# Three issuers changed in one trunk layer: pins out of the DeltaNet heads, x1 stores and operand-set loads on GpSimd

## The chip, the cores and the metric

The kernel runs on one core of a Trainium2 chip. The metric is device time of one launch in microseconds. Three runs of the kernel before gave 1958.57, 1965.72 and 1967.81 us (median 1965.72). One more execution was recorded by the hardware profiler; every row below is from it.

## The reference

One decoder layer on x of 1024 positions by 1024 channels, all in float32:

```
h = rmsnorm(x, norm1_g) * (1 + scale1(c)) + shift1(c)
x = x + gate1(c) * hybrid_mixer(h)          # DeltaNet, pooling, spatial gating, retention, gates, w_out
h = rmsnorm(x, norm2_g) * (1 + scale2(c)) + shift2(c)
x = x + gate2(c) * (square(relu(h @ mlp_w1)) @ mlp_w2)
out = rmsnorm(x, final_g)
```

The mixer's DeltaNet has 4 heads of 128 channels; for each, q, k and v pass a causal convolution, then a chunked gated delta rule with a triangular solve per chunk of 64. The MLP widens 1024 channels to 4096 and back.

## The kernel before, in words

The work runs in stages on one core: modulation and the pooling and spatial branches (to about 200 us), the four DeltaNet heads (to about 545), retention (710), the sigmoid gates (1020), the branch products (1205), the output projection (to 1297), and the MLP (to the end). Channels lie on partitions and positions along the free axis, in two halves of 512.

A float32 product is made as three fp32r matmuls: each operand is cast to a high part by ScalarE and the rest subtracted by VectorE (`split` and `put`, lines L112 and L113, and L967 and L968). In the MLP one level of Strassen is used on top: 7 products of 12 matmuls each take the place of 8. Its operands, sums and differences of the four quarters, are "operand sets": b11, b21, n2, t3, n1, t4, b22.

**The order of the work.** Program order on each engine is set by a scheduler that knows data, slots and costs. `keep_in_program_order` holds an instruction where the source writes it (a "pin"). `fill(n)` takes n matmuls (L424) from a projection that has nothing to do with this head, and writes them there, so that TensorE has work while the head's chain on VectorE and ScalarE goes on. In `dn_mix` 10 fillers stand ahead of the pinned key transposes (L575), and in head 0 another 28 ahead of the pinned key-query products (L615). L601 are the key-key products, L608 the value transposes, L591 the VectorE step that scales the transposed keys `kt` and frees their bank. `dn_inverse` is the triangular solve, a row of 31 pairs of small VectorE instructions (L652 and L656); for the next head its first pair is made before the scan of the head at hand (`next(nxt)`), and pinned.

**The output projection** (`outproj`) makes for each half eight blocks of x1: load the residual `xr` (L1200), multiply, add on VectorE (L1204), store x1 to DRAM for later (L1206). All DMAs there are issued by SyncE in one queue, which goes on to the loads of the MLP's first weights, `raw<-in_w` (L1250). `xr` and the squares of the norm share a ring of slots named "st", six or seven tiles of 128x512.

**The MLP** makes 16 panels of the hidden activation (`up`), and stores the seven operand sets of each panel to DRAM (`ad_b`, `ad_n`, `ad_t`, L1285; their names in the trace merge b11, b21 and b22, n1 and n2, t3 and t4). Its second product (`down`) runs over four chunks c of four panels, and within a chunk over four output blocks m; the seven sets of a chunk stay in SBUF for its four blocks. While the last block of a chunk is multiplied, each set that has been used up is replaced by that of the next chunk: 4 loads of 256 KB (L1414, tile `ar`, in the six slots of "st"), each cast on ScalarE (L967) and subtracted on VectorE (L968). Such a "turn" has 28 loads; there are four, in panel 15 for chunk 0 and in the last blocks of chunks 0, 1 and 2, and 112 loads in all. SyncE issues them in one queue with the stores of the sets (L1285), the weight loads (L1250) and, in chunk 1, the reloads of x1 (L1536).

Of the kernel before, what the change touches and what calls it, by code (L numbers as in the profile page):

```python
# [13 lines left out]
ALU = mybir.AluOpType  # L14

P = 128
# [84 lines left out]
class Trunk:  # L101
# [460 lines left out]
    def dn_mix(self, h, q, kT, vT, Es):  # L562
        nc, mp = self.nc, self.mp
        sm = lambda n: mp.tile([P, 8], FP32, tag=n, name=n, bufs=2)
        kk, qq, bb, bk, nn, tmp = sm("kk"), sm("qq"), sm("bb"), sm("bk"), sm("nn"), sm("nt")
        kt = mp.tile([P, NB, P], FP32, tag="kt", name="kt", bufs=2)
        nv = mp.tile([P, NB, P], FP32, tag="vt", name="nv", bufs=2)
        N3 = mp.tile([P, NB, P], FP32, tag="N3", name="N3", bufs=2)
        Ab = mp.tile([P, NB, P], FP32, tag="Ab", name="Ab", bufs=2)
        cb = lambda t, c: t[:, c * P:(c + 1) * P]  # L570
        qT = q[3][1]
        pks = [self.pss() for _ in range(2)]
        self.fill(10)
        for c in range(NB):
            i = nc.tensor.transpose(out=pks[c // 4][:, c % 4 * P:(c % 4 + 1) * P], in_=cb(kT, c), identity=self.ident)  # L575
            if c == 0:
                self.tc.keep_in_program_order(i)
        for c in range(NB):
            junk = mp.tile([P, P], FP32, tag="junk", name="junk", bufs=1)
            nc.scalar.activation(out=junk, in_=pks[c // 4][:, c % 4 * P:(c % 4 + 1) * P], func=AF.Square,  # L580
                                 accum_out=kk[:, c:c + 1])
        q[2]()
        q2 = mp.tile([P, T], FP32, tag="r4", name="q2", bufs=3)
        nc.scalar.activation(out=q2, in_=qT, func=AF.Square)
        nc.vector.tensor_scalar_add(out=kk, in0=kk, scalar1=EPS)
        nc.vector.reciprocal(out=bb, in_=kk)
        nc.vector.tensor_tensor(out=bb, in0=bb, in1=self.beta[:, h], op=ALU.mult)
        nc.vector.tensor_tensor(out=bk, in0=bb, in1=self.ekl[:, h], op=ALU.mult)
        for hf in range(2):
            c4 = slice(4 * hf, 4 * hf + 4)  # L590
            nc.vector.tensor_tensor(out=kt[:, c4], in0=pks[hf].rearrange("p (c d) -> p c d", c=4),  # L591
                                    in1=self.b4(bk[:, c4]), op=ALU.mult)
            nc.gpsimd.tensor_tensor(out=Es[hf], in0=Es[hf], in1=self.b4(bb[:, c4]), op=ALU.mult)
        self.rsqrt(kk, nn, tmp)
        nc.vector.tensor_tensor(out=nn, in0=nn, in1=kk, op=ALU.mult)
        for hf in range(2):
            c4 = slice(4 * hf, 4 * hf + 4)
            ch = range(4 * hf, 4 * hf + 4)
            p1 = self.pss()
            for j in range(4):  # L600
                nc.tensor.matmul(out=p1[:, j * P:(j + 1) * P], lhsT=cb(kT, ch[j]), rhs=cb(kT, ch[j]), start=True, stop=True)  # L601
            nc.vector.tensor_tensor(out=N3[:, c4], in0=p1.rearrange("p (c i) -> p c i", c=4), in1=Es[hf], op=ALU.mult)
        for hf in range(2):
            c4 = slice(4 * hf, 4 * hf + 4)
            ch = range(4 * hf, 4 * hf + 4)
            pv = self.psm()
            for j in range(4):
                nc.tensor.transpose(out=pv[:, j * P:(j + 1) * P], in_=cb(vT, ch[j]), identity=self.ident)  # L608
            nc.vector.tensor_tensor(out=nv[:, c4], in0=pv.rearrange("p (c d) -> p c d", c=4), in1=self.b4(nn[:, c4]),
                                    op=ALU.mult)  # L610
            p2 = self.pss()
            if h == 0 and hf == 0:
                self.fill(28)
            for j in range(4):
                i = nc.tensor.matmul(out=p2[:, j * P:(j + 1) * P], lhsT=cb(kT, ch[j]), rhs=cb(qT, ch[j]), start=True,  # L615
                                     stop=True)
                if h == 0 and hf == 0 and j == 0:
                    self.tc.keep_in_program_order(i)
            nc.vector.tensor_tensor(out=Ab[:, c4], in0=p2.rearrange("p (c i) -> p c i", c=4), in1=Es[hf], op=ALU.mult)
        self.drain()  # L620
        for hf in range(2):
            sl = slice(hf * 512, (hf + 1) * 512)
            qs = [mp.tile([P, 512], FR, tag="w5", name=n, bufs=4) for n in ("qh", "ql")]
            self.split(q2[:, sl], *qs)
            pq = self.pss()
            for i, r in enumerate(qs):
                nc.tensor.matmul(out=pq[0:1], lhsT=self.oner, rhs=r, start=(i == 0), stop=(i == 1))
            nc.scalar.copy(out=q2[0:1, sl], in_=pq[0:1])
        qd = self.dp.tile([1, T], FP32, tag="qd", name="qd", bufs=2)
        nc.sync.dma_start(out=qd, in_=q2[0:1])  # L630
        nc.sync.dma_start(out=qq, in_=qd.rearrange("o (c p) -> (o p) c", p=P))

        nr = mp.tile([P, 32, 32], FP32, tag="nr", name="nr")
        nd = self.dp.tile([4, 8, 32, 32], FP32, tag="nd", name="nd", bufs=2)
        for b in range(4):
            nc.sync.dma_start(out=nd[b].rearrange("c j i -> j c i"), in_=N3[b * 32:b * 32 + 32, :, b * 32:b * 32 + 32])
        nc.sync.dma_start(out=nr.rearrange("p j i -> p (j i)"),
                          in_=nd.rearrange("b c j i -> (b c) (j i)").unsqueeze(0).broadcast_to([4, 32, 1024]))
        return dict(h=h, q=qT, k=kT, kt=kt, nv=nv, N3=N3, Ab=Ab, qq=qq, nr=nr)

    def dn_inverse(self, s):

        nc, mp = self.nc, self.mp
# [5 lines left out]
        for j in range(31):  # L649
            m = 31 - j  # L650
            tmp = mp.tile([P, 31, 8], FP32, tag="ttm", name="ttm", bufs=1)
            i = nc.vector.tensor_tensor(out=tmp[:, :m], in0=nr[:, j, j + 1:].unsqueeze(2).broadcast_to([P, m, 8]),  # L652
                                        in1=tt[:, j:j + 1].broadcast_to([P, m, 8]), op=ALU.mult)
            if j == 0 and s["h"]:
                self.tc.keep_in_program_order(i)
            nc.vector.tensor_tensor(out=tt[:, j + 1:], in0=tt[:, j + 1:], in1=tmp[:, :m], op=ALU.subtract)  # L656
            yield
        t2 = mp.tile([P, 8, 32], FP32, tag="t2", name="t2")
# [213 lines left out]
    def mixers(self):  # L872
# [22 lines left out]
        self.fillers = [vn[0]]  # L895
        st = self.dn_mix(0, q, k[3][1], v[3][1], E)
        prev = None
        nxt = self.dn_inverse(st)
        for h in range(4):
            inv = nxt  # L900
            hooks = {}
            if prev:
                hooks[12] = lambda: self.mix_out(0, h - 1, *prev)
            if h < 3:
                k, q = self.dn_proj(1, h + 1), self.dn_proj(0, h + 1)
                v = vn
                v[1]()
                hooks[30] = v[2]
                self.run(k[0], hooks, inv, 2)
                k[1]()  # L910
                self.run(q[0], {12: k[2]}, inv, 2)
                for _ in inv:
                    pass
                q[1]()
                E = self.dn_decay(h + 1)
                z, zg = self.gate_in(DZ + h)
                self.fillers = [zg]
                sn = self.dn_mix(h + 1, q, k[3][1], v[3][1], E)
                vn = self.dn_proj(2, h + 2) if h < 2 else self.ret_proj(2, 0)
                self.fillers = [vn[0]]  # L920
            else:
                rk, rq = self.ret_proj(1, 0), self.ret_proj(0, 0)
                self.run(rk[0], hooks, inv, 2)
                self.run(rq[0], {}, inv, 2)
                for _ in inv:
                    pass
                z, zg = self.gate_in(DZ + h)
                self.fillers = [zg]
            self.dn_levels(st)
            if h < 3:  # L930
                nxt = self.dn_inverse(sn)
                next(nxt)
            prev = self.dn_scan(h, st), self.prm[:, R_DNG:R_DNG + 1], z
            if h < 3:
                st = sn
# [250 lines left out]
    def outproj(self):  # L1186
# [7 lines left out]
        for hf in range(2):  # L1194
            x1 = self.x1[hf] = self.xb.tile([P, NB, 512], FP32, tag="b16", name="x1", bufs=4)
            ssq = self.st("ssq")
            for db in range(NB):
# [5 lines left out]
                         [self.ml[hf][:, k] for k in range(NB)])  # L1203
                nc.vector.scalar_tensor_tensor(out=x1[:, db], in0=ps, scalar=self.modc[:, 16 + db:17 + db], in1=xr,  # L1204
                                               op0=ALU.mult, op1=ALU.add)
                nc.sync.dma_start(out=self.x1d[hf][db], in_=x1[:, db])  # L1206
                self.sumsq(x1[:, db], ssq, db, nc.vector if db == NB - 1 else nc.gpsimd)
                if hf == 1:
                    self.h2_first(db, rs)
# [63 lines left out]
    def mlp(self):  # L1273
# [134 lines left out]
        def load(c, o):  # L1408
# [2 lines left out]
                self.S2[o] = self.opset(pool, tag, 1 if tag == "ex" else 4)  # L1411
            for j in range(4):
                r = self.st("ar")
                nc.sync.dma_start(out=r, in_=ad[o, 4 * c + j])  # L1414
                self.put(self.S2[o], j, r)

        for p in range(NP):
# [232 lines left out]
```

## Time and profile before

| | before |
|---|---|
| runs, us | 1958.57, 1965.72, 1967.81 |
| profiled execution, us | 1969.17 |
| its span, us | 1967.3 |
| mean granted TensorE clock | 0.980 |
| TensorE matmul busy | 1878.3 us, 95% |
| VectorE busy | 1343.7 us, 68% |
| ScalarE busy | 762.5 us, 39% |
| GpSimd busy | 116.5 us, 6% |

Busy time is the time in which an engine had an instruction under way. "PE" is TensorE's matmuls, "DVE" VectorE, "ACT" ScalarE, "POOL" GpSimd, "SP" SyncE, and "SPq" its queue of DMA issues. PEclk is the granted share of TensorE's full clock; at half of it a busy engine does half of the work. A row "A <- B" says that A's idle time ended with B.

### The profile page before, as it was taken

The page shows a single profiled execution, that of the slowest core. Times are in us where ns is not written, and L with a number is a line of the kernel's source. Part 1 is how long each engine was busy: PE and PEld are TensorE (multiplying, and loading weights), DVE is VectorE, ACT ScalarE, POOL GpSimd, SP SyncE. Part 2 cuts the span into 40 slices and gives each one's busy share as a digit, 9 for nine tenths or more (in the row PEclk, how much of TensorE's full clock was granted, in tenths as well). Part 3 has the DMA queues.
Part 4 walks back from the last instruction along what each step waited for, and adds up shares of the span by engine and source line. Part 5 has one row for each costly group of instructions (what it writes and reads, how often), then busy time and mean ns, then how long its engine had stood idle before and what let it go on. Part 6 is the DMA issues. An engine that isn't in the chain of part 4 may idle for free.

```text
span 1967.3 us, 24099 instructions
## 1 busy us (share of the span) xinstructions
PE 1878.3 (95%) x8888; PEld 1537.7 (78%) x8888; DVE 1343.7 (68%) x2337; ACT 762.5 (39%) x1214; POOL 116.5 (6%) x105
## 2 busy tenths in 40 slices
PE   5999989999999998999999999989999999999997
PEld 2788867777788887888878888878778877787875
DVE  7844687787454468566655776558886666788785
ACT  4523543442312134434442123545234444635542
POOL 4100300210000000000000000200000000000000
PEclk9999999998899999999999999999999999999998
DMA  7522111231122224454448653535664564535422
GB/s 267 185 98 86 53 37 45 60 84 48 49 75 61 68 102 160 150 182 166 166 157 267 197 191 130 182 134 177 200 203 133 185 199 155 204 131 190 151 85 86
DMA packets 142225, 270.67 MB, mean 138 GB/s; under 512 B 45078, under 2 KB 45718, under 8 KB 138012
## 3 DMA queue, kind: packets, MB, share of 16 engines
q1 hardware_dynamic: 140188, 262.85, 40.1%
q0 software_dynamic: 1920, 6.29, 1.3%
q8 instruction: 69, 1.13, 0.2%
q14 instruction: 48, 0.39, 0.1%
HBM read 198.30 MB, written 66.60 MB: 135 GB/s over the span
## 4 chain that ended last, share of the span: by engine, by line
PE 42%; DMA 5%; DVE 4%; issue 2%; ACT 2%; SPq 0%; DVEq 0%; ACTq 0%
PE sm L985 14%; PE mm L985 14%; PE mm L128 9%; PE sm L128 4%; DMA ar<-ad_b 2%; DVE op L968 1%; DVE x L1277 1%; DMA ar<-ad_t 1%; DVE x L1276 1%; ACT op L967 1%; DMA ar<-ad_n 1%; DVE raw L1256 1%; DMA raw<-in_w 1%; DVE dl L113 0%; DMA adaw<-in_ada 0%
## 5 line engine op out<-in xcount | busy, mean ns | idle before, releaser
L424 PE MATMUL mm<-hh,wlo 128*128 128x512 f32 x512 | 207.4, 405 | 0.0
L424 PE MATMUL mm<-hl,whi 128*128 128x512 f32 x512 | 206.9, 404 | 0.0
L424 PE MATMUL mm<-hh,whi 128*128 128x512 f32 x512 | 206.8, 404 | 0.0
L113 DVE TENSOR_TENSOR wlo<-raw,whi 128x1024 fp32r<-128x1024 f32 x71 | 87.6, 1236 | 96.4 <-ACT whi L112 95.6
L112 ACT CAST whi<-raw 128x1024 fp32r<-128x1024 f32 x73 | 76.5, 1050 | 178.5 <-PE mm L424 109.8
L985 PE MATMUL sm<-op,ch 128*128 128x512 f32 x392 | 123.1, 395 | 1.7 <-ACT v L1487 1.7
L985 PE MATMUL mm<-op,gh 128*128 128x512 f32 x352 | 112.8, 400 | 9.2 <-ACT x L1368 4.9
L424 PEld LDWEIGHTS mm<-hh,whi 128*128 128x128 f32 x512 | 98.4, 192 | 18.1 <-issue 0.3
L424 PEld LDWEIGHTS mm<-hh,wlo 128*128 128x128 f32 x512 | 98.4, 192 | 17.6
L424 PEld LDWEIGHTS mm<-hl,whi 128*128 128x128 f32 x512 | 98.1, 192 | 17.8
L112 ACT CAST gh<-raw 128x1024 fp32r<-128x1024 f32 x58 | 61.1, 1053 | 113.3 <-PE sm L985 72.9
L985 PE MATMUL sm<-op,gh 128*128 128x512 f32 x328 | 102.3, 393 | 2.6 <-DVE x L1276 1.5
L112 ACT CAST ch<-raw 128x1024 fp32r<-128x1024 f32 x57 | 60.0, 1053 | 85.7 <-PE sm L985 48.9
L985 PEld LDWEIGHTS sm<-op,ch 128*128 128x128 f32 x392 | 73.7, 190 | 19.8 <-ACT v L1487 2.6
L985 PEld LDWEIGHTS mm<-op,gh 128*128 128x128 f32 x352 | 67.0, 192 | 26.1 <-ACT x L1368 5.8
L985 PE MATMUL mm<-op,ch 128*128 128x512 f32 x272 | 84.9, 394 | 0.0
L1256 DVE TENSOR_TENSOR raw<-raw 128x512 f32<-128x512 f32 (+1 forms) x96 | 83.2, 866 | 1.6
L968 DVE TENSOR_TENSOR op<-ar,op 128x512 fp32r<-128x512 f32 x112 | 72.1, 687 | 16.6 <-ACT op L967 16.3
L113 DVE TENSOR_TENSOR cl<-raw,ch 128x1024 fp32r<-128x1024 f32 x57 | 69.6, 1222 | 18.2 <-ACT ch L112 17.8
L985 PE MATMUL sm<-op,cl 128*128 128x512 f32 x196 | 77.2, 394 | 0.6 <-DVE cl L113 0.6
L967 ACT CAST op<-ar 128x512 fp32r<-128x512 f32 x112 | 66.2, 618 | 29.2 <-DMA ar<-ad_b 16.3
L985 PEld LDWEIGHTS sm<-op,gh 128*128 128x128 f32 x328 | 60.8, 188 | 18.6 <-DVE x L1276 4.0
(463 smaller groups left out, 4671.9 us busy)
## 6 DMA issues: line engine op xcount, KB each, us to landing
raw<-in_wt SPq DMA_DIRECT2D x80, 512.0 KB, 5.3
raw<-in_w SPq DMA_DIRECT2D x32, 1024.0 KB, 4.8
adaw<-in_ada SPq DMA_DIRECT2D x64, 256.0 KB, 5.6
sig<-sg SPq DMA_DIRECT2D x64, 256.0 KB, 2.7
sg<-x SPq DMA_DIRECT2D x60, 256.0 KB, 2.2
ad_b<-x SPq DMA_DIRECT2D x48, 256.0 KB, 2.3
ar<-ad_b SPq DMA_DIRECT2D x48, 256.0 KB, 5.4
adaw<-in_ada SPq DMA_DIRECT2D x16, 512.0 KB, 7.1
```

The source lines that it names most:

```text
L112: nc.scalar.copy(out=hi, in_=raw)
L113: (eng or nc.vector).tensor_tensor(out=lo, in0=raw, in1=hi.bitcast(FP32), op=ALU.subtract)
L128: self.nc.tensor.matmul(out=ps, lhsT=a, rhs=b, start=(i == 0), stop=(i == 3 * n - 1))
L424: self.nc.tensor.matmul(out=ps, lhsT=blk(a, k), rhs=r[hf][:, k], start=(k == 0 and i == 0), stop=(k == NB - 1 and i == 2))
L967: self.nc.scalar.copy(out=hi, in_=x)
L968: self.nc.vector.tensor_tensor(out=lo, in0=x, in1=hi.bitcast(FP32), op=ALU.subtract)
L985: self.nc.tensor.matmul(out=ps, lhsT=a, rhs=b, start=start and n == 0, stop=(n == 11), skip_group_check=True)
L1256: add = lambda o, a, b: nc.vector.tensor_tensor(out=o, in0=a, in1=b, op=ALU.add)
L1276: tt = lambda eng, o, a, b, op: eng.tensor_tensor(out=o, in0=a, in1=b, op=op)
L1277: stt = lambda o, a, s, b, op0, op1: nc.vector.scalar_tensor_tensor(out=o, in0=a, scalar=s, in1=b, op0=op0, op1=op1)
```

## The change

(A) `fill(10)` and `fill(28)` go, with the pins on L575, L615 and the first solve pair; the next head's solve is no longer started ahead of the scan. (B) The 16 stores of x1 are issued by GpSimd. (C) So are the 112 loads of operand sets.

```
@@ dn_mix
-        self.fill(10)
         for c in range(NB):
-            i = nc.tensor.transpose(out=pks[c // 4][:, c % 4 * P:(c % 4 + 1) * P], in_=cb(kT, c), identity=self.ident)
-            if c == 0:
-                self.tc.keep_in_program_order(i)
+            nc.tensor.transpose(out=pks[c // 4][:, c % 4 * P:(c % 4 + 1) * P], in_=cb(kT, c), identity=self.ident)
...
-            if h == 0 and hf == 0:
-                self.fill(28)
             for j in range(4):
-                i = nc.tensor.matmul(out=p2[:, j * P:(j + 1) * P], lhsT=cb(kT, ch[j]), rhs=cb(qT, ch[j]), start=True,
-                                     stop=True)
-                if h == 0 and hf == 0 and j == 0:
-                    self.tc.keep_in_program_order(i)
+                nc.tensor.matmul(out=p2[:, j * P:(j + 1) * P], lhsT=cb(kT, ch[j]), rhs=cb(qT, ch[j]), start=True, stop=True)
@@ dn_inverse
-            if j == 0 and s["h"]:
-                self.tc.keep_in_program_order(i)
@@ heads
-        nxt = self.dn_inverse(st)
         for h in range(4):
-            inv = nxt
+            inv = self.dn_inverse(st)
...
-            if h < 3:
-                nxt = self.dn_inverse(sn)
-                next(nxt)
@@ outproj
-                nc.sync.dma_start(out=self.x1d[hf][db], in_=x1[:, db])
+                nc.gpsimd.dma_start(out=self.x1d[hf][db], in_=x1[:, db])
@@ mlp, load
-                nc.sync.dma_start(out=r, in_=ad[o, 4 * c + j])
+                nc.gpsimd.dma_start(out=r, in_=ad[o, 4 * c + j])
```

Line numbers after the change are lower: L575, L601, L608 and L615 become L574, L598, L605 and L610; L1200, L1206 and L1250 become L1186, L1192 and L1236; L1285 and L1414 become L1271 and L1400.

In the heads, TensorE's order in head 0 before; the names `hh`, `hl`, `whi` and `wlo` are those of the fillers, and L627 is the next step of the head:

```order
L424 MATMUL mm<-hh,whi 128x512
L575 MATMUL sm<-cst,cv 128x128 x8
L601 MATMUL sm<-cv 128x128 x8
L608 MATMUL mm<-cst,cv 128x128 x4
L424 MATMUL mm<-hl,whi 128x512
...
L615 MATMUL sm<-cv 128x128 x4
L608 MATMUL mm<-cst,cv 128x128 x4
L615 MATMUL sm<-cv 128x128 x4
```

and the same place after:

```order
L574 MATMUL sm<-cst,cv 128x128 x8
L605 MATMUL mm<-cst,cv 128x128 x8
L424 MATMUL mm<-hh,whi 128x512
...
L598 MATMUL sm<-cv 128x128 x8
L424 MATMUL mm<-hh,wlo 128x512
...
L610 MATMUL sm<-cv 128x128 x8
```

Before, 10 fillers stand ahead of the transposes and 28 between L608 and L615 (12 there in head 1). After, none stands ahead, 5 stand ahead of the key-key products and 17 between these and L610, in heads 0, 1 and 3 alike. The count of matmuls is the same.

At the end of the output projection, SyncE's queue before:

```order
L1206 DMA x1d_4_9913<-x_10241 128x512
L1200 DMA xr<-in_xT 128x512
L1206 DMA x1d_5_9914<-x_10241 128x512
L1200 DMA xr<-in_xT 128x512
L1206 DMA x1d_6_9915<-x_10241 128x512
L1200 DMA xr<-in_xT 128x512
L1206 DMA x1d_7_9916<-x_10241 128x512
L1250 DMA raw<-in_w 128x1024 x5
```

and after:

```order
L1186 DMA xr<-in_xT 128x512
L117 DMA raw<-in_wo 128x1024
L1186 DMA xr<-in_xT 128x512 x3
L1236 DMA raw<-in_w 128x1024 x5
L1271 DMA ad_b_0_10582<-x_10781 128x512
```

The stores x1d have left the queue, so that the last three residual loads stand together and the first MLP weights right behind them.

In panel 15, where the sets of chunk 0 are loaded, SyncE's queue before (`ad_b_15`, `ad_n_15` and `ad_t_15` are the stores of that panel, `sums` and `x` their sources):

```order
L1414 DMA ar<-ad_t_2_10664 128x512
L1285 DMA ad_b_15_10693<-x_13027 128x512
L1414 DMA ar<-ad_t_3_10665 128x512
L1414 DMA ar<-ad_b_0_10678 128x512
L1414 DMA ar<-ad_b_1_10679 128x512
L1285 DMA ad_b_15_10613<-x_12996 128x512
L1250 DMA raw<-in_w 128x2048
L1414 DMA ar<-ad_b_2_10680 128x512
L1414 DMA ar<-ad_b_3_10681 128x512
L1285 DMA ad_n_15_10661<-sums 128x512
```

and after:

```order
L1271 DMA ad_b_15_10597<-x_12923 128x512
L1271 DMA ad_b_15_10693<-x_13027 128x512
L1271 DMA ad_b_15_10613<-x_12996 128x512
L1236 DMA raw<-in_w 128x2048
L1271 DMA ad_n_15_10661<-sums 128x512
```

The loads stand in GpSimd's queue after, in the same order among themselves, with nothing between them up to the end of the MLP. The chunk in each number is the first figure behind the name: `ad_t_2` is panel 2.

## Rows read from the trace of the kernel before

**Rows 1.** The page: busy time by engine, and the software DMA queue.
```profile
PE 1878.3 (95%) x8888; PEld 1537.7 (78%) x8888; DVE 1343.7 (68%) x2337; ACT 762.5 (39%) x1214; POOL 116.5 (6%) x105
...
q0 software_dynamic: 1920, 6.29, 1.3%
```
**Rows 2.** Waits of TensorE, 1440 to 1900 us: total, times, longest.
```profile
PE mm L985 <- ACT x L1368: 4.9, 1, 4.9
PE mm L985 <- DVE al L113: 3.9, 1, 3.9
PE sm L985 <- ACT v L1487: 2.8, 3, 1.1
PE mm L985 <- ACT v L1487: 0.9, 1, 0.9
PE mm L985 <- ACT x L1484: 0.9, 1, 0.9
```
**Rows 3.** Windows: length, busy time and count by engine, PEclk, DMA share, GB/s.
```profile
1608.00:1618.00 10.00, 6.32 (x28) 4.88 (x26) 4.74 (x7) 6.00 (x11) 0.00 (x0) 1.00 0.85 296
1618.00:1626.00 8.00, 6.09 (x15) 4.31 (x16) 4.09 (x7) 3.99 (x8) 0.00 (x0) 0.57 0.41 131
1626.00:1636.00 10.00, 10.00 (x45) 7.98 (x44) 9.08 (x14) 6.23 (x11) 0.00 (x0) 1.00 0.59 203
1790.00:1796.00 6.00, 3.20 (x15) 2.31 (x13) 5.92 (x10) 4.28 (x7) 0.00 (x0) 0.98 0.91 324
1796.00:1803.00 7.00, 5.87 (x15) 4.67 (x16) 6.58 (x9) 0.00 (x0) 0.00 (x0) 0.53 0.35 135
```
**Rows 4.** The chain of waits up to the first turn's stall: start, length, what.
```profile
1602.14 0.45 issue
1602.59 0.70 DVE sums L1277
...
1603.31 0.32 SPq L1285
...
1603.68 6.15 DMA ar<-ad_b
...
1610.47 0.54 ACT x L1282
...
1611.03 0.32 SPq L1285
...
1611.45 4.07 DMA ar<-ad_n
```
**Rows 5.** The chain of waits, 1772 to 1802 us, by line.
```profile
by line: DMA ar<-ad_b 36.5%; DVE op L968 18.6%; DMA ar<-ad_t 11.5%; DMA ar<-ad_n 10.9%; PE sm L985 10.0%; PE mm L985 6.9%; ACT op L967 6.3%; issue 5.4%; DVE al L113 3.8%; ACT v L1487 2.3%; DVE x L1276 2.2%; DVEq L968 0.2%; ACTq L1487 0.1%
```
**Rows 6.** Tile ar: its casts, and microseconds from issue to landing of its loads.
```profile
L967 ACT CAST op<-ar x112: 604/621/627, 1562.0 to 1877.1; 128x512 fp32r<-128x512 f32 x112
L968 DVE TENSOR_TENSOR op<-ar,op x112: 681/685/694, 1563.5 to 1878.1; 128x512 fp32r<-128x512 f32 x112
...
DMA to landing us min/median/max: 2.7/4.0/6.1
```
**Rows 7.** Tiles hr, then sw, which GpSimd loads: issue, VectorE beside it, landing.
```profile
L1024 DVE TENSOR_TENSOR hr<-hr x8: 684/685/692, 714.5 to 742.8; 128x512 f32<-128x512 f32 x8
...
L1048 POOL DMA_DIRECT2D hr<-hd x4: 548/548/577, 660.4 to 734.7; - x4
...
DMA to landing us min/median/max: 2.9/3.0/4.2
...
DMA to landing us min/median/max: 3.0/3.6/6.6
```
**Rows 8.** Timeline of the output projection's end: start, length, engine, line.
```profile
1281.07 0.33 SPq L1206 DMA_DIRECT2D x1d<-x  x1
...
1297.76 8.35 SPq L1250 DMA_DIRECT2D raw<-in_w  x4
...
1300.02 0.26 ACT L1580 ACTIVATE rt<-mm,eps 128x4 f32<-128x4 f32 x1 [1.94 <-PE mm L1571]
...
1302.01 1.04 ACT L112 CAST ah<-raw 128x1024 fp32r<-128x1024 f32 x1 [1.73 <-DMA raw<-in_w]
...
1303.11 1.22 PE L985 MATMUL sm<-op,ah 128*128 128x512 f32 x2 [3.13 <-ACT ah L112]
```
**Rows 9.** Waits of TensorE in the heads, 200 to 545 us, and a window.
```profile
PE sm L615 <- DVE kt L591: 8.4, 2, 6.2
PE sm L681 <- DVE XX L687: 3.5, 1, 3.5
PE sm L601 <- ACT E L557: 2.1, 1, 2.1
...
276.00:284.00 8.00, 3.52 (x17) 3.55 (x18) 7.69 (x30) 2.73 (x3) 2.11 (x2) 0.57 0.02 4
```

More of the change, by code (lines that the diff above doesn't have):

```diff
@@ L638, in dn_mix @@
                           in_=nd.rearrange("b c j i -> (b c) (j i)").unsqueeze(0).broadcast_to([4, 32, 1024]))
-        return dict(h=h, q=qT, k=kT, kt=kt, nv=nv, N3=N3, Ab=Ab, qq=qq, nr=nr)
+        return dict(q=qT, k=kT, kt=kt, nv=nv, N3=N3, Ab=Ab, qq=qq, nr=nr)
     def dn_inverse(self, s):
@@ L651, in dn_inverse @@
             tmp = mp.tile([P, 31, 8], FP32, tag="ttm", name="ttm", bufs=1)
-            i = nc.vector.tensor_tensor(out=tmp[:, :m], in0=nr[:, j, j + 1:].unsqueeze(2).broadcast_to([P, m, 8]),
-                                        in1=tt[:, j:j + 1].broadcast_to([P, m, 8]), op=ALU.mult)
-            if j == 0 and s["h"]:
-                self.tc.keep_in_program_order(i)
+            nc.vector.tensor_tensor(out=tmp[:, :m], in0=nr[:, j, j + 1:].unsqueeze(2).broadcast_to([P, m, 8]),
+                                    in1=tt[:, j:j + 1].broadcast_to([P, m, 8]), op=ALU.mult)
             nc.vector.tensor_tensor(out=tt[:, j + 1:], in0=tt[:, j + 1:], in1=tmp[:, :m], op=ALU.subtract)
```

## The prediction

> **What bounds the kernel now.** I read the page first: TensorE is busy 1878.3 of 1967.3 us [rows 1]. So nothing that stays beside its matmuls can be worth much, and a gain has to come out of the 89 us in which it is idle or out of stretches at a low clock. Then TensorE's waits for the stages that the change touches, then windows around the longest ones, and last the chain of waits that leads up to them.
>
> In the MLP's second product the waits are few: 4.9, 3.9, 2.8, 0.9 and 0.9 us, 13.4 together [rows 2]. The two long ones cost more than they last. A full window of 10 us holds 45 matmuls, 0.222 us each. The 18 us from 1608 to 1626 hold 28 + 15 = 43 where 81 would fit, and the second of these windows was granted a clock of 0.57, the 1.2 GHz level for most of it, after the engine had stood still for 4.9 us. So this stall costs 38 x 0.222 = 8.4 us. The same for 1790 to 1803: 30 of 58, at 0.53 in its second part, 28 x 0.222 = 6.2 us [rows 3]. With the three short groups (2.8 + 0.9 + 0.9 = 4.6 us) the four turns cost 8.4 + 6.2 + 4.6 = 19.2 us. That is the ceiling for (C).
>
> **(C), the 112 loads.** What makes the first stall is the chain before it [rows 4]: a load of `ar` waits to be issued behind a store of panel 15 in SyncE's queue, and that store waits for VectorE or ScalarE, which is itself behind the cast of an earlier `ar`. The queue so turns a wait for a store into a wait for a load. From 1602.14 to 1603.68 (1.54 us) and from 1610.47 to 1611.45 (0.98 us) the chain goes through a store and not through a load, a cast or a slot: 2.5 us that GpSimd's queue, which has no store in it, doesn't have to wait. The load that lands late under this is one of six slots, and the later ones start from it, so 2.5 us is the least that comes off if landing times stay. With the stall cut from 4.9 to 2.4 us or less part of the slow clock goes too (8.4 - 4.9 = 3.5 us of the cost lie there). I take 2.5 + 3.5 = 6 us; bounds 2.5 and 8.4.
>
> At the second stall the chain is another one: 36.5 + 11.5 + 10.9 = 59% of it is landings of `ar`, and VectorE's `op` L968 another 19%; no store and no SyncE step appears in it [rows 5]. It is bound by six slots: a slot is taken for 4.0 us of landing, 0.62 of cast and 0.69 of subtraction, 5.3 us [rows 6], so 28 loads take at least 28 x 5.3 / 6 = 24.7 us, where seven products want 84 x 0.222 = 18.6. A new issuer adds no slot. It changes the landing alone: loads that GpSimd issues took 3.0 (hr) and 3.6 us (sw) as a median [rows 7] against 4.0. At 3.6 a turn takes 28 x 4.9 / 6 = 22.9 us, 1.8 less, at 3.0 it takes 20.1, 4.6 less; but hr and sw flew in stages with less other traffic, so I take a little under the smaller: 1.5 us for the second stall and 1 us for the short ones together. Bounds: the whole 10.8 us that they cost, and for the other side the worst landing of sw, 6.6 us, 28 x 2.6 / 6 = 12 us more in each of the three turns of `down`, 36 us in all.
>
> The issue itself costs GpSimd 548 ns a load [rows 7], 28 x 0.55 = 15.3 us in a turn, under the 18.6 us of its products, and GpSimd has nothing else to do there (0.00 busy [rows 3]). SyncE loses 28 issues a turn; its stores and weight loads go earlier, and may crowd the DMA engines (0.85 and 0.91 busy in the two bad windows [rows 3]); that is in the bound above. Sum for (C): -6 - 1.5 - 1 = -8.5 us.
>
> VectorE ran beside GpSimd's loads without stretching: its hr instructions took 684 to 692 ns there [rows 7], the same as L968's 681 to 694 without GpSimd [rows 6]. The Trainium skill (SBUF — State Buffer, the box "The DVE blocks DMA trap" in the section "SBUF: two separate sides") holds the opposite danger: GpSimd writes its DMAs' descriptors itself, and can't while VectorE runs an instruction in a two-port mode. By that rule loads would land late in the turns, and (C) would turn into a loss. The 3.0 and 3.6 us speak against it, though the 6.6 us at worst leaves it open; it is the first rival below. The skill also says (DMA: Bandwidth & Descriptors, "Issuing engines are not separate DMA queues") that a second issuer saves only sequencer time, small beside the transfer. By that rule (C) would be worth about nothing; here the sequencer's time is that of waits in order, and the 2.5 us of the first chain are of this kind.
>
> **(B), the 16 stores.** Before, SyncE's last store of x1 waits for the last block, and so the first MLP weights are issued at 1297.76 and used at 1302.01, 4.25 us later. After, the queue holds before them only three residual loads, the last of which takes the slot of the block whose store went at 1281.07. So the weights are issued some 15 us earlier and lie there. What ends last is then ScalarE's root at 1300.02, done at 1300.28; the cast starts there instead of at 1302.01, and TensorE's first product, which waits for that cast, 1.7 us before 1303.11 [rows 8]. The stores cost GpSimd 16 x 0.55 = 9 us beside its sums of squares, which have some 5.6 us from one block to the next (from the fifth store at 1281.07 to the queue's step past the eighth at 1297.76 [rows 8]). Gain 1.7 us; bounds 0 and 3.1 (the whole wait).
>
> **(A), the heads.** The matmuls stay; what matters is how many of them cover the chain up to `kt`. TensorE waited for it twice, 8.4 us, and the longest, 6.2 us, left a window at a clock of 0.57 [rows 9]. In head 1 10 + 12 = 22 fillers stood ahead of L615 before, and 5 + 17 = 22 stand there after. TensorE gets there at the same time, and VectorE, busy 7.69 of 8 us in that window, sets when `kt` is ready: no change. The 2.1 us wait of L601 gets 5 fillers, 1.1 us, ahead of it, but they are taken from what covers L615. In head 0 38 become 22, 16 x 0.222 = 3.6 us less cover, while the transposes start 10 x 0.222 = 2.2 us earlier; at most 1.4 us is short there. The early solve pair is one instruction of 62. I take 0; bounds: a gain of the two waits and the slow clock behind the longer (8.4 + 0.43 x 8 = 11.8 us), or a loss of one more such stall, 6.2 + 3.4 = 9.6 us.
>
> **The sum.** -8.5 - 1.7 + 0 = -10.2 us against the profiled execution's 1969.17, 1959.0 us. That execution lies 3.45 us above the median of the runs, and above the highest of them; the change is the same step from either, so I forecast from the median: 1965.7 - 10.2 = 1955.5 us.
>
> **Rivals.**
> 1. GpSimd's loads land later (slower). From 4.0 us each further microsecond costs a turn 28 / 6 = 4.7 us, the three turns of `down` 14 us. It decides from a landing of 4.0 + 10.2 / 14 = 4.7 us: above that the gain of all parts is gone. At 6 us, 28 - 10.2 = 18 us slower, 1983. For it: sw's worst of 6.6, DMA engines 0.85 to 0.91 busy there. Against: the medians 3.0 and 3.6. Chance 0.14.
> 2. The heads get longer (slower). One more stall such as that of head 1, 9.6 us, in two heads, 19 - 10 = 9 us slower, 1975. For it: in head 0 the cover shrinks. Against: the count of 22 in head 1 and a chain on VectorE that no filler moves. Chance 0.08.
> 3. No change: slots bound every turn, and the head of the queue was not what held the loads. Only (B) is left, 1964. For it: 59% landings in the second chain [rows 5]. Against: the two stores in the first [rows 4]. Chance 0.23.
> 4. The loads run so far ahead that every turn is covered: 19.2 + 1.7 = 21 us, 1945. For it: two of the four turns share less than the 4.6 us of short waits already [rows 2]. Against: 24.7 us of slots for 18.6 us of products. Chance 0.15.
>
> **How the numbers follow.** The forecast has 0.40: a gain of 5 to 15 us, 1951 to 1961. About 0.5%, 9.8 us, is what a measurement of this kernel can tell from no change; it cuts the forecast's case through the middle. Faster by more: 0.23 of the forecast, 0.15 of rival 4, and 0.05 of rival 3 where (A) gains; 0.43. Within: 0.17 of the forecast, 0.18 of rival 3, 0.04 of rivals 1 and 2; 0.39. Slower: the rest, 0.18. The range takes in rivals 3 and 4 and a part of 1 and 2: 1942 to 1976. The forecast's own is 1951 to 1961.
>
> **What would show it.** In the profile after: the wait of about 4.9 us on x at the end of panel 15 gone or halved, with the clock of that stretch near 1; landings of `ar` at 3.0 to 4.0 us; the second turn (about 1790) still with a wait for `al` or a cast; the first MLP weights issued some 15 us before the output projection's end and ScalarE's cast right behind the root; waits for `kt` of 8 us in total in the heads. It is wrong if `ar` lands at 4.7 us or later, if VectorE's L968 grows beyond 694 ns, or if the heads' waits grow by more than 4 us.

## The result, and the profile after

The changed kernel takes 1976.31 us as a median of 20 runs, the kernel before 1965.44 in the same runs; the ratio is 1.0056 [1.0043, 1.0069]. It is slower by 11 us where 10.2 us less were forecast, and the time lies 0.3 us above the range of 1942 to 1976. One of the 20 runs took 2334.68 us at a granted clock of 0.752; the ratio leaves it out. The profiled execution took 1971.79 us (span 1970.0).

The two profiled executions are 2.7 us apart, and that hides most of the loss. The one after reaches TensorE's first product of the MLP 10.4 us earlier (1292.67 against 1303.11). Only 1.8 us of this come from (B). Most of the rest is a stretch from 500 to 600 us that ran at a granted clock of 0.93 before and at 1.00 after (541 and 571 matmuls in it). From that first product to the end the MLP took 664.2 us before and 677.3 after, 13.1 us more.

The page after, answering to [rows 1]:

```profile
PE 1875.1 (95%) x8888; PEld 1532.6 (78%) x8888; DVE 1345.2 (68%) x2337; ACT 764.1 (39%) x1214; POOL 186.3 (9%) x233
...
q0 software_dynamic: 12160, 39.86, 6.4%
```

TensorE has the same work, and GpSimd has its 128 DMAs more. TensorE's waits from 1440 to 1900 us, answering to [rows 2]:

```profile
PE mm L971 <- ACT x L1354: 5.9, 2, 4.1
PE sm L971 <- ACT v L1473: 4.4, 4, 1.8
PE mm L971 <- ACT ah L112: 3.1, 1, 3.1
PE mm L971 <- ACT x L1470: 2.9, 2, 2.1
PE mm L971 <- ACT v L1473: 2.8, 2, 2.2
PE sm L971 <- DVE gl L113: 1.7, 1, 1.7
PE sm L971 <- DVE cl L113: 1.1, 2, 0.6
...
```

All rows of this view add up to 22.7 us here and to 14.9 before. The long wait at panel 15 is 4.1 us where it was 4.9, a wait of 3.1 us for a cast (`ah`) stands near 1795 where the 3.9 stood, and several waits of 1 to 2 us for ScalarE's evictions (its copies of products out of TensorE's banks) are new.

Windows, answering to [rows 3], round the first turn's stall:

```profile
1598.00:1608.00 10.00, 6.88 (x31) 5.36 (x29) 5.59 (x9) 4.84 (x9) 3.21 (x6) 0.94 0.97 345
1608.00:1615.00 7.00, 6.01 (x17) 4.84 (x18) 2.86 (x5) 3.83 (x7) 2.23 (x5) 0.60 0.65 206
```

The granted clock falls to 0.60 behind the first stall, the 1.2 GHz level for most of it, as it did before (0.57). The DMA engines are 0.97 busy ahead of it, against 0.85. The loads of `ar`, answering to [rows 6]:

```profile
L953 ACT CAST op<-ar x112: 603/620/627, 1552.1 to 1876.8; 128x512 fp32r<-128x512 f32 x112
L954 DVE TENSOR_TENSOR op<-ar,op x112: 680/691/695, 1554.9 to 1877.6; 128x512 fp32r<-128x512 f32 x112
...
DMA to landing us min/median/max: 2.8/4.0/6.8
```

They land in 4.0 us as a median, as before. (Of SyncE's 112 loads before, the trace has only 14 landings, so this compares few with many.) The output projection's end, answering to [rows 8], and one wait of the heads, answering to [rows 9]:

```profile
1272.84 22.53 SPq L1236 DMA_DIRECT2D raw<-in_w  x4
...
1291.42 0.26 ACT L1566 ACTIVATE rt<-mm,eps 128x4 f32<-128x4 f32 x1 [1.94 <-PE mm L1557]
1291.58 1.03 ACT L112 CAST ah<-raw 128x1024 fp32r<-128x1024 f32 x1
...
1292.67 1.12 PE L971 MATMUL sm<-op,ah 128*128 128x512 f32 x2 [1.29 <-ACT ah L112]
```

```profile
PE sm L610 <- DVE kt L588: 8.1, 2, 6.0
```

Both are as the prediction has them: the first weights are issued from 1272.84, 18.7 us ahead of their cast, the cast stands right behind the root, TensorE waits 1.29 us where it waited 3.13, and the heads' waits for `kt` stay.

**Where the first stall comes from now.** ScalarE's timeline in panel 15 after, and GpSimd's queue:

```profile
1605.86 0.62 ACT L953 CAST op<-ar 128x512 fp32r<-128x512 f32 x1 [1.66 <-DMA ar<-ad_n]
1606.78 0.62 ACT L953 CAST op<-ar 128x512 fp32r<-128x512 f32 x1 [0.31 <-DMA ar<-ad_n]
1607.83 0.62 ACT L953 CAST op<-ar 128x512 fp32r<-128x512 f32 x1 [0.43 <-DMA ar<-ad_t]
1608.36 0.58 ACT L1354 COPY x<-mm 128x512 f32<-128x512 f32 x1
```

```profile
1596.41 1.15 POOL L1400 DMA_DIRECT2D ar<-ad_n  x2 [0.78 <-DVE op L954]
1601.95 1.08 POOL L1400 DMA_DIRECT2D ar<-ad_n  x2 [4.40 <-DVE op L954]
```

TensorE waits for the eviction L1354. It stands in ScalarE's order behind three casts, each of which starts as its load lands; those loads were issued at 1601.95 and after, when slots came free. The slots came free late because loads 6 to 9, which had them, were slow. (Loads are counted from 0 here.) They were issued some 10 matmuls earlier than before, from 1593.76 on, but at a DMA share of 0.97 they took 5.9 to 6.5 us to land. So six slots hold the turn, without any store in the queue.

### The profile page after: what moved, and what is told of

Its sections match the earlier page's. It is cut to its first block, busy times and chain, and to the rows that moved or that the text cites. A ratio compares the mean times of both kernels' runs of the same rounds, so it can differ in the third digit from the quotient of the medians.

```text
span 1970.0 us, 24187 instructions
## 1 busy us (share of the span) xinstructions
PE 1875.1 (95%) x8888; PEld 1532.6 (78%) x8888; DVE 1345.2 (68%) x2337; ACT 764.1 (39%) x1214; POOL 186.3 (9%) x233
## 5 line engine op out<-in xcount | busy, mean ns | idle before, releaser
L954 DVE TENSOR_TENSOR op<-ar,op 128x512 fp32r<-128x512 f32 x112 | 73.8, 688 | 25.0 <-ACT op L953 24.4
```

The lines of the kernel that those rows point to most:

```text
L954: self.nc.vector.tensor_tensor(out=lo, in0=x, in1=hi.bitcast(FP32), op=ALU.subtract)
```

## The experiments

Each of these kernels ran 5 to 12 times; a ratio is to the kernel before, measured beside it on the same chip, with its 95% interval.

**The three parts alone, and two of them.** e1 has the edits of `dn_mix`, `dn_inverse` and `heads`; e2 has

```
-                nc.sync.dma_start(out=self.x1d[hf][db], in_=x1[:, db])
+                nc.gpsimd.dma_start(out=self.x1d[hf][db], in_=x1[:, db])
```

e3 has the edit of `load`; e4 is e1 and e2 together.

> Part (A) alone. Theory 1 (the loss lies in the operand-set loads): the profile of the changed kernel is some 7 us ahead at 520 us, where a stretch at half clock is missing, so this kernel is -7 to +1 us against before. Theory 2 (the heads got longer without the pins, and the profiled execution was a lucky one): +5 to +12 us, with longer TensorE waits or more half clock between 200 and 545 us.

> Part (B) alone. TensorE's, ScalarE's and VectorE's orders are those of before, only SyncE's and GpSimd's queues differ. Both theories: -1 to -3 us, the first cast of the MLP right behind ScalarE's root. If it is slower by over 2 us, the stores on GpSimd are a cost that neither theory has.

> Part (C) alone. Theory 1: +10 to +16 us, all of it behind 1540 us, in TensorE's waits at the turns. Theory 2: -8 to +2 us.

> (A) and (B) without (C). Theory 1: -2 to -10 us, faster than before and 12 to 20 us faster than the changed kernel. Theory 2: +3 to +10 us.

Measured: e1 0.9986 [0.9971, 1.0001], e2 1.0000 [0.9986, 1.0014], e3 1.0053 [1.0035, 1.0071], e4 0.9983 [0.9966, 1.0000]. (C) is the whole loss: e3 has it without (A) and (B), and e4, which has both without (C), loses nothing.

**Issuer or order?** The scheduler places casts and evictions elsewhere when the loads change their queue. e5 takes (C) and holds TensorE's, ScalarE's and VectorE's orders to those of before by edges that cost no semaphore; e6 leaves the loads on SyncE and holds the orders to those of (C).

```
e5: -   nc.sync.dma_start(out=r, in_=ad[o, 4 * c + j])
    +   nc.gpsimd.dma_start(out=r, in_=ad[o, 4 * c + j])
e5, e6: +   self.follow(ORDER)        # b behind a, on one engine
```

> (C) alone, but TensorE, ScalarE and VectorE are held to the order of before from panel 13 on (a list of places, no wait added); GpSimd issues the loads. Theory 1a (the scheduler's new order of casts and evictions on ScalarE makes the loss): within 3 us of before or faster, since the loads are free of SyncE's stores and the order is the old one. Theory 1b (GpSimd as issuer makes the loss, by issue time, landing or its reaction to a released slot): +8 to +14 us as (C) alone.

> The kernel before, SyncE issues the loads, but TensorE, ScalarE and VectorE are held to the order that they have in (C) alone. Theory 1a: +8 to +14 us, the waits for ScalarE's evictions (L1368, L1487) as in (C) alone. Theory 1b: within 3 us of before.

Measured: e5 1.0044 [1.0026, 1.0061], e6 1.0028 [1.0010, 1.0045]. Either alone costs; e6's 5.5 us lie between what its two theories gave. The two make 0.72% together where e3, which has both, lost 0.53%; at these intervals that is no difference. Slots are the same for all 112 loads in e5 and before. (Both hold the orders from panel 13 on.)

**Which turns?** Orders as before; only some loads on GpSimd:

```
e7: +   (nc.gpsimd if c == 0 else nc.sync).dma_start(out=r, ...)
e8: +   (nc.gpsimd if c > 0 else nc.sync).dma_start(out=r, ...)
```

> GpSimd issues the 28 loads of chunk 0 alone (in panels 13 to 15), the other 84 stay on SyncE; TensorE, ScalarE and VectorE are held to the order of before. Theory 1b' (a slot of the ring that comes free is reused 0.27 us later by GpSimd, 0.30 us against SyncE's 0.03 in the profiles, and each turn goes through the ring 28/6 = 4.7 times, so every turn loses some 1.3 us and a little slow clock): +1 to +3 us. Rival (what hurts is only that the loads of panel 15 are taken out of SyncE's queue between its stores): +6 to +10 us here and nothing in the next kernel.

> The other way round: the 84 loads of chunks 1 to 3 by GpSimd, those of chunk 0 by SyncE, order of before. Theory 1b': three turns, +4 to +8 us. Rival: within 2 us of before.

Measured: e7 1.0001 [0.9986, 1.0016], e8 1.0032 [1.0013, 1.0050]. In e7's profile the wait at panel 15 is still there:

```profile
PE mm L992 <- ACT x L1375: 4.3, 1, 4.3
```

With no store ahead of its loads the first turn gains nothing, and it loses nothing either, where 1 to 3 us were expected. The loss comes with the loads of chunks 1 to 3, those of the turns in `down`; it need not lie within these turns, as is seen below.

**A seventh slot.** e9 takes (A) and (B), and makes room for a seventh tile in "st" by moving small tiles to other pools; e10 adds (C). e11 is e9 with the small tile `a1` left in its old pool; e12 is e11 with (C), its orders held to e11's. The lines are drawn together from the edits:

```
e9:  -   self.one, gtr, oner, wba, tk, a1 = cp.tile(...)
     +   self.one, gtr, oner, wba, tk, a1 = self.cq.tile(...)
     -   self.nst = 6
     +   self.nst = 7
e11: +   self.a1 = cp.tile(...)       # as before
```

> (A) and (B) without (C), and the ring st of the MLP with seven slots for six (512 B tiles of constants that the MLP doesn't need go into an earlier pool). If the ring bounds the turns (28 x 5.3 / 6 = 24.7 us against 28 x 5.3 / 7 = 21.2), the four turns lose less: -6 to -14 us against before, -4 to -10 against (A) and (B) with six slots. If the ring is not the limit: -1 to -4 us against before.

> The whole change with seven slots. Ring theory: the extra slot hides the late reuse, so most of the 11 us that the change costs goes: -6 to +3 us against before. If the loss has nothing to do with the ring, it stays: +7 to +12 us.

> As with seven slots on SyncE, but one tile of 32 B stays where it was, so that every operand tile of the left side starts at a multiple of 64 B again, as in the kernel before; with seven slots so far they started at 32 beyond one, and a full window of 50 us held 216 matmuls instead of 222, in stages too that the ring has no part in. If the address does that: 222 again from 800 us on, and with the turns' waits gone, as they were there, -14 to -22 us against before. If the lower rate has another cause: +8 to +14 us as before.

> The same kernel with the loads on GpSimd, and TensorE, ScalarE and VectorE held to the order of that kernel. Theory 1b' (the late reuse of a slot matters because the ring bounds the turn): within 4 us of the kernel with SyncE. If GpSimd's loads are slow in a way that no slot hides (landing, weight loads and stores that now collide with them): 8 to 16 us slower than it.

Measured: e9 1.0068 [1.0050, 1.0086], e10 1.0166 [1.0143, 1.0189], e11 0.9902 [0.9884, 0.9920] (1946.59 us), e12 0.9985 [0.9969, 1.0001]. e11 beats both kernels. e9 and e10 missed what was expected of them, by over 15 us each: the move of `a1` had a cost of its own, which the last section takes up. e11's waits of 1440 to 1900 us add up to 8.3 us; the longest groups:

```profile
PE sm L973 <- ACT v L1475: 4.3, 4, 1.5
PE sm L973 <- ACT x L1472: 1.9, 1, 1.9
```

So slots were the bound. Against e4, which has (A) and (B) with six slots, the seventh is worth 0.81%, some 16 us, the scheduler's new order for seven slots included. That is most of the 19.2 us which the prediction counted for the four turns; 8.3 us of waits are left. But with the same seven slots and the same orders, GpSimd still costs 0.83%: that a slot more would hide its slower start is wrong.

**The start of each load.** e13 and e14 leave SyncE as the issuer, and let GpSimd write one column of the slot first; e17 and e18 have three such memsets. Orders and slots are unchanged.

```
e13 (on before), e14 (on e11): +   nc.gpsimd.memset(r[:, 0:1], 0.0)
e17, e18: +   for q in range(3): nc.gpsimd.memset(r[:, q:q + 1], 0.0)
                nc.sync.dma_start(out=r, in_=ad[o, 4 * c + j])
```

> The kernel before, with SyncE as the issuer of the 112 loads and the orders of TensorE, ScalarE, VectorE and SyncE all unchanged, and the same slot for each load. New is one GpSimd memset of one column of the slot ahead of each load: GpSimd waits for the slot to come free, and SyncE waits for GpSimd. So SyncE's queue stays as it is, and only the time from a slot's release to the issue of the next load grows, by GpSimd's reaction (0.29 us in place of 0.03) and the memset. Theory of the reaction (GpSimd's loads cost time because GpSimd takes longer to notice a free slot): slower by about as much as the experiment in which GpSimd issues the loads in the order of before, ratio 1.003 to 1.006, 6 to 12 us. Rival (it is GpSimd's DMA path, or that its loads go ahead of the stores and weight loads): no change, 0.998 to 1.0015.

> The same memset ahead of each load in the version with seven slots and SyncE as the issuer (0.9902), again with the orders of all engines and the slots unchanged. Theory of the reaction: most of the 16 us by which GpSimd's loads are slower than SyncE's there come back, ratio 0.994 to 0.999. Rival (DMA path, or loads that run ahead): 0.989 to 0.992.

> As the relay, with three memsets of 98 ns in place of one ahead of each of SyncE's loads: some 0.35 to 0.4 us from a slot's release to the issue, where one memset gave 0.18, SyncE alone 0.03 and GpSimd as issuer 0.30 (and 0.05 us more of landing). Engines' orders and slots are those of before. Theory that GpSimd's cost beside the pause is the later start of each load: about the 1.0031 of GpSimd with the pause moved, 1.002 to 1.004. Rival (something else in GpSimd's queue, such as loads that go ahead of stores and weights): 0.999 to 1.0015.

> The same in the version with seven slots (0.9902 with SyncE, 0.9925 with one memset, 0.9971 with GpSimd and the pause moved). Theory of the later start: 0.995 to 0.998. Rival: 0.990 to 0.994.

Measured: e13 1.0010 [0.9992, 1.0027], e14 0.9925 [0.9899, 0.9951], e17 1.0014 [0.9998, 1.0030], e18 0.9925 [0.9908, 0.9942]. In e17 a load goes out some 0.25 us behind the release of its slot, which is nearly GpSimd's 0.30. This part of the delay is worth 0.14% (six slots) and 0.23% (seven), each within the error of nothing, and less than the 0.44% and 0.83% of GpSimd. So the theory that the later start makes the loss missed: e13, e17 and e18 came out where its rivals had them, and e14 just above that.

**A pause.** In every profile with at least 121 DMAs of GpSimd, seven of them, one load goes out 3.04 us behind the event that frees its slot, where the others go out 0.29 to 0.30 behind. The kernel after, GpSimd's queue and VectorE at the end of the third turn:

```profile
1783.59 1.21 POOL L1400 DMA_DIRECT2D ar<-ad_t  x2 [1.02 <-DVE op L954]
1788.28 2.17 POOL L1400 DMA_DIRECT2D ar<-ad_b  x4 [3.49 <-DVE op L954]
```

```profile
1784.55 1.33 DVE L954 TENSOR_TENSOR op<-ar,op 128x512 fp32r<-128x512 f32 x2 [0.59 <-ACT op L953]
...
1792.17 0.69 DVE L954 TENSOR_TENSOR op<-ar,op 128x512 fp32r<-128x512 f32 x1 [2.10 <-ACT op L953]
```

The load at 1788.28 is load 80. It takes the slot of load 74, which the first of the two instructions at 1784.55 frees at 1785.24, 3.04 us earlier. The row names only the line of its releaser, L954; which instruction of that line it was follows from the slot. GpSimd's DMAs up to there, by the groups of its instructions after (16 + 8 + 8 + 4 + 4 = 40, and 80 loads):

```profile
L1192 POOL DMA_DIRECT2D x1d<-x x16 | 8.9, 554 | 532.1 <-DVE x L1190 532.1
L790 POOL DMA_DIRECT2D sw<-rraw x8 | 4.3, 532 | 206.3 <-ACT rraw L786 206.3
L791 POOL DMA_DIRECT2D sw<-rraw x8 | 4.1, 517 | 0.0
L1034 POOL DMA_DIRECT2D hr<-hd x4 | 2.2, 553 | 69.0 <-ACT zT L534 49.5 <-DVE op L954 19.4
L1035 POOL DMA_DIRECT2D hr<-hd x4 | 2.2, 549 | 2.8 <-DVE op L954 1.5 <-DVE hl L954 1.3
```

So it is the 121st. In e10 and e12, which have the 16 stores too, it is load 80 again, 3.04 us behind its slot; in e3 and e5, without them, load 96, also by 3.04 us and also the 121st. e8 has 108 DMAs and no such load. e5, GpSimd and VectorE:

```profile
1861.91 1.15 POOL L1421 DMA_DIRECT2D ar<-ad_n  x2 [3.90 <-DVE op L975]
1866.45 2.17 POOL L1421 DMA_DIRECT2D ar<-ad_t  x4 [3.40 <-DVE op L975]
```

```profile
1860.92 2.49 DVE L975 TENSOR_TENSOR op<-ar,op 128x512 fp32r<-128x512 f32 x4
```

The first row is an undisturbed one: the first of VectorE's four ends at 1861.61, and GpSimd issues 0.30 us later. The slot of the load at 1866.45 is freed by the fourth, at 1863.41. e15 and e16 move the pause: 12 of the 16 stores of x1 go to GpSimd, so that the 121st DMA is load 84, issued 30 us (e16: 40) ahead of its cast. Otherwise e15 is e5, and e16 is e12.

```
+ (nc.gpsimd if hf or db > 3 else nc.sync).dma_start(out=self.x1d[hf][db], ...)
```

> In every profile in which GpSimd issues the loads and at least 121 DMAs in all, its 121st DMA starts about 3.04 us later than the release of its slot and the end of the issue before it allow: load 96 where only the loads moved (24 DMAs of the stages before + 96), load 80 where the 16 stores of x1 moved too. Both stand in the middle of a turn. Here, beside the 112 loads in the order of before, 12 of the 16 stores of x1 are issued by GpSimd, so that the 121st DMA is load 84, the first of chunk 3, which is issued some 30 us before its cast. Theory of the pause (it falls by count, and what it hits decides what it costs): no load of a turn is late by 3 us, load 84 takes the pause, and the ratio is 1.000 to 1.0025, against 1.0044 with the pause at load 96. Rivals: the pause belongs to that place in the turn and stays at load 96; or it goes and the time stays at 1.0035 to 1.006, then it was not the cost.

> The same for the version with seven slots: GpSimd issues the 112 loads in the orders of the SyncE version, and 12 of the 16 stores of x1 where it issued 16 (SyncE the first 4), so that the 121st DMA moves from load 80 to load 84. Theory of the pause: the TensorE wait of 4.6 us on ScalarE's v near 1787 is gone, ratio 0.990 to 0.995 where it was 0.9985 with the pause at load 80 and 0.9902 with SyncE. Rival: 0.997 to 1.000.

Measured: e15 1.0031 [1.0013, 1.0048], e16 0.9971 [0.9951, 0.9992]. The pause went where the count says. In e15, VectorE frees the slot of load 84 at 1820.22, and the load goes out 3.05 us later (e16: 3.04):

```profile
1819.54 0.68 DVE L1283 TENSOR_TENSOR x<-x,v 128x512 f32<-128x512 f32 x1
```

```profile
1823.27 0.56 POOL L1421 DMA_DIRECT2D ar<-ad_b  x1 [28.19 <-DVE raw L1263]
```

And it left its old place; load 96 of e15:

```profile
1861.79 2.49 DVE L975 TENSOR_TENSOR op<-ar,op 128x512 fp32r<-128x512 f32 x4
```

```profile
1864.58 0.55 POOL L1421 DMA_DIRECT2D ar<-ad_t  x1 [0.66 <-DVE op L975]
```

It goes out 0.30 us behind the fourth (1861.79 + 2.49 = 1864.28). That the pause follows the count is shown. Its price is not: the ratios fall by 0.13 and 0.14%, in the same direction both times, but less than the interval of each. Both came out above the range that the theory gave, and e16's in that of its rival. In the MLP of the profiles the move is worth 3.0 us with six slots and 8.0 with seven (next table).

**The MLP by itself.** The MLP starts between 1289.6 and 1304.8 us in these profiles, by what the stages ahead of it happened to take, and that blurs the totals. This is its own length, from TensorE's first product to the end of the span, in one profile of each kernel:

| loads of the sets | six slots, us | seven slots, us |
|---|---|---|
| SyncE | before 664.2, e1 664.2, e2 664.1, e4 664.5 | e11 652.0 |
| SyncE, later start | e13 664.4, e17 664.7 | e14 650.6, e18 652.5 |
| SyncE, orders of (C) | e6 669.2 | |
| GpSimd, first turn alone | e7 664.5 | |
| GpSimd, old orders | e5 674.1, without the first turn e8 671.4 | e12 664.8 |
| the same, pause moved | e15 671.1 | e16 656.8 |
| GpSimd, new orders | e3 672.9, after 677.3 | |

By this measure the first turn and the later start cost 0.5 us at most, and the seventh slot gains 12.5 us over e4. GpSimd with the old orders costs 9.9 us with six slots and 12.8 with seven; with the pause moved 6.9 and 4.8 are left.

**Where the rest lies.** The largest single step of that rest stands right behind the first turn, where `down` begins. Its first evictions write to the place where the `sums` of panel 15 lay, and so they wait until SyncE's last store of `sums` has landed. e11, by SyncE's queue, ScalarE and a window:

```profile
1629.05 0.32 SPq L1273 DMA_DIRECT2D ad_t<-sums  x1
```

```profile
1631.95 0.69 ACT L1472 ACTIVATE x<-mm,ng 128x512 f32<-128x512 f32 x1 [2.67 <-DVE al L113]
```

```profile
1628.00:1643.00 15.00, 14.54 (x63) 11.37 (x62) 9.79 (x12) 4.69 (x6) 0.00 (x0) 1.00 0.53 172
```

The same in e16:

```profile
1625.33 0.32 SPq L1280 DMA_DIRECT2D ad_t<-sums  x1
```

```profile
1631.77 0.69 ACT L1479 ACTIVATE x<-mm,ng 128x512 f32<-128x512 f32 x1 [6.22 <-DMA ad_t<-sums]
```

```profile
1628.00:1643.00 15.00, 11.82 (x46) 9.07 (x45) 6.07 (x8) 3.52 (x5) 0.55 (x1) 0.89 0.23 88
```

With SyncE as the issuer, the store took at most 2.9 us to land. With GpSimd five of chunk 1's first six loads went out ahead of it, and it took 6.4 us. TensorE waited 3.2 us for the eviction, the clock behind that was lower, and 17 matmuls (3.8 us at 0.222) are missing from the window. e12 has the same wait of 3.2 us; e5, e8 and e15 wait 2.2, 2.0 and 2.0 us at this place, with a granted clock of 0.66, 0.77 and 0.77 from 1650 to 1655, where it was 1.00 before. This is read from the traces; no run moved these six loads alone.

## Why the prediction was wrong

**(A), right within the error.** Forecast 0; e1 gives -0.14%, no more than its error, and the wait for `kt` is 8.1 us for 8.4. A small gain is possible: the clock from 500 to 600 us was 0.93 to 0.95 in 7 of 10 profiled executions without (A), and 1.00 in 9 of 10 with it.

**(B), right in the profile, and too small to see.** The mechanism came as described and 1.84 us of the wait went; 1.7 were forecast. e2's ratio of 1.0000 has room for that.

**(C), the failing step.** The forecast of -8.5 us came out as +10 (e3's ratio; its MLP is 8.7 us longer).
- Its largest term, -6, rests on the sentence that 2.5 us "is the least that comes off" since GpSimd's queue has no store in it. The stores are gone from the queue, and the stall went from 4.9 to 4.1 us, with the slow clock behind it as before. e7 measures this term alone: nothing (1.0001; the MLP 664.5 us for 664.2). A chain shows what came last, not what stands right behind it; the loads went earlier, landed later at a DMA share of 0.97, and waited for the same six slots.
- The terms -1.5 and -1 rest on "A new issuer adds no slot. It changes the landing alone". The first half is right: slots were the bound, and e11, one slot more, gains 19 to 20 us together with (A) and (B). The second half is wrong. The median landing stayed at 4.0 us, where these terms go by the 3.0 and 3.6 of other loads; other things changed. They are the engines' orders (e6, +0.28%); the time from a free slot to the issue, 0.30 us for 0.03 (about e17's +0.14%, within its error); the pause (0.13% by the ratios, less than their error, and 3 us in the MLP); and SyncE's last stores, which land later beside loads that no longer stand behind them. The prediction named that crowding, but left it to its bound and put nothing for it into the sum.
- None of its signs of being wrong came clearly: `ar` landed at 4.0 us, L954 took 691 ns as a median and 695 at most where 694 was the mark, and the heads' waits did not grow. The two signs for (C) watched the loads' landing and VectorE, and the loss lay in neither.
- Rival 1, the slower one, named a landing above 4.7 us as its condition. Landings were 4.0, so the loss came by another way than the rival's. Rival 3 had the reason why nothing is gained, not why something is lost.

What the pause does to TensorE shows in e12. Its longest wait is for an eviction, which stands in ScalarE's order behind the casts of loads 80 to 83, the paused one and those behind it. In e16, with the pause moved, the longest of this group is 1.7 us. e12 and then e16:

```profile
PE sm L980 <- ACT v L1482: 8.5, 4, 4.6
```

```profile
PE sm L980 <- ACT v L1482: 5.0, 4, 1.7
```

The Trainium skill (DMA: Bandwidth & Descriptors, "Issuing engines are not separate DMA queues") says that a second issuer saves only sequencer time, which is small. The prediction set it aside for the 2.5 us of the chain; e7's 1.0001 agrees with the rule. The loss in e5 and e8 lies beyond it.

**Open.** With the pause moved, GpSimd costs 0.31% and 0.69% (0.9971 against 0.9902); a delay of nearly its size on SyncE's loads costs 0.14% and 0.23%. Some 0.17 and 0.46% are left, at errors of about 0.25 each, so the first is not clear of nothing. In the MLP's lengths 6.4 us (e15 against e17) and 4.3 us (e16 against e18) are left. With seven slots the late store behind panel 15 accounts for most of that; with six for a part. That chunk 1's first loads are what delays it was not tried by itself, nor were the loads that go ahead of stores and weight loads elsewhere, up to 70 matmuls earlier in e5 (first loads of chunk 3). Why the 121st DMA pauses is not known either.

## What to carry to other kernels

Before a stall is put down to the head of a queue, ask what the freed instruction will wait for next: here it was slots, and one slot more was worth what a new issuer was not. An issuer has properties of its own (its reaction, its pauses, the order that the scheduler makes of it, the transfers that its own now run beside); price them from its rows in the trace, in stages as tight as the one it is moved to. Where stages ahead of the changed one vary between executions, compare the length of the changed stage rather than the total. An engine that casts and evicts in one order hands every late load on to TensorE.

## What was not expected of the hardware

- GpSimd issued a waiting DMA 0.29 to 0.30 us behind the event that released it, SyncE 0.03, while GpSimd's own memset started 0.05 us behind it: in e13 a memset and SyncE's issue behind it take 0.18 us together.
- The 121st DMA of GpSimd started 3.04 us behind the release of its slot, in seven profiles of seven.
- A store of SyncE's took 6.4 us to land with five loads of GpSimd's issued in the 3.4 us before it (e16), and at most 2.9 us with two (e11).
- The start of TensorE's operand tiles counts. In e9 the tiles of one side of SBUF, which hold the activations among TensorE's operands, begin 32 bytes past a multiple of 64, in e11 on one; nothing else differs but the place of a tile of 8 columns, `a1`, whose move shifts them. The orders of all engines are the same. Only this one shift was tried. The same window of the gates' stage, e9 and then e11:

```profile
850.00:900.00 50.00, 50.00 (x215) 40.03 (x214) 32.51 (x53) 21.48 (x31) 0.00 (x0) 1.00 0.47 157
```

```profile
850.00:900.00 50.00, 50.00 (x221) 41.09 (x220) 29.42 (x45) 19.73 (x29) 0.00 (x0) 1.00 0.48 161
```

At full clock and without a wait, 215 matmuls go through in 50 us, against 221: 2.7% of the rate, and 1.7% of the whole time (1.0068 against 0.9902).
